# A seventh-product pair more, a fourth raw buffer, two reordered output blocks and spread transposes in a two-layer hybrid encoder

## The chip, the cores and the metric

The kernel runs on one core of one Trainium2 chip, as one program. Its time is the device time of one execution in microseconds. The kernel before has a median of 2345.92 us over three runs (2344.45 to 2348.73). Everything is float32; matrix products are taken as three products of a high and a low part in the fp32r type.

## The reference

Two layers, each of three residual sub-layers on 512 tokens of width 1024. Cut to what matters here:

```
h = h + 0.5 * post(SwiGLU(pre(h)))                 # FFN 1, hidden width 2816
u = pre(h); proj = u @ w_in
qa, ka, va, qb, kb, vb, qc, kc, vc, gl = split(proj)
  A: neighbourhood attention, 8 heads, with a bias table per head
  B: sliding-window attention, 8 query heads, 2 key heads, rotary, sink logit
  C: differential attention, 4 heads, two softmax maps each, rotary
gates = sigmoid(gl + b_gate)                       # 3 branches x 1024 columns
merged = sum_n gates[n] * (branch_n @ w_branch[n])
h = h + post(merged @ w_out)
h = h + 0.5 * post(SwiGLU(pre(h)))                 # FFN 2
```

All weights are read once from DRAM, 128x128 blocks in the order in which the kernel uses them. `gl` makes 24 column blocks of 128: 8 for each branch, called ga0 to ga7, gb0 to gb7 and gc0 to gc7 below.

## The kernel before, in words

Activations are held transposed, 1024 features by 512 tokens. Each layer goes through the stages FFN 1, projection (`project`), mixer (`mixer`) and FFN 2. TensorE is named PE below, VectorE DVE, ScalarE ACT, GpSimd POOL; SP is the queue that issues most transfers.

**Two ways to make a column block.** The direct way (`dense`, `mm3`, L322 to L324) takes eight row blocks of the weight, three products each, on 512 tokens: 24 matmuls of 512 columns for a column block of 128. The other way (`Seven`) takes a pair of column blocks together, as a two-by-two matrix of quadrants, by seven products in place of eight (Strassen's scheme in Winograd's form). Each product is 12 matmuls of 256 columns (`product`, L687), so a pair is 84 matmuls. For it the weights are added and split on DVE and ACT first: `sum13` (L628), `high1`, `low1` (L637), `high13`, `low13` (L647), `sum2` (L651), `high12` (L657), `low12` (L661), `sum4` (L665), `high24` (L669) and `low24` (L674). The accumulators are read back by `seed` (L726), `copy7` (L731), `copy2` (L735), `add21` (L740) and `add22` (L745). The loop over groups is a software pipeline: while group g is multiplied, group g+1 is prepared and the weights of group g+2 are asked for.

**Raw weights** come in tiles of 512 KB into a ring `wr` of three buffers (`fetch`, L206). A group takes two of them. A buffer comes free when the last of these DVE and ACT instructions has read it.

**The projection** makes 6 column blocks directly and 13 pairs by `Seven`: 12 pairs of q, k and v, and the pair gc6, gc7. Results are turned, rotated or split on DVE and ACT in tiles of a ring `t` of 16 buffers of 2 KB a partition, and stored to DRAM by POOL. `tables_of_a` also loads what the first two bias tables of attention A need; `biases` builds them (L1750, in tiles `edges`).

**The mixer** follows a written order, the string `ORDER`: qa0, aa0 and so on load and run attention heads, ga0 is a directly made gate block, fc0 to fc3 finish the four heads of attention C, and ya, yb, yc multiply a branch's output by a column block of `w_branch`. A gate block is 24 matmuls of 512 columns, a y block 12. A tile scheduler orders the instructions of each engine by this order and by when it takes operands to be ready, so gates and y blocks stand between the pieces of the attention heads. Gates of the branches B and C are stored to DRAM and read back when their y block is due.

**The first FFN** also keeps x: `keep` (L908 to L911) turns hT back by transposes on PE into a single PSUM bank `o`, ACT evicts it into a tile of the ring `t` of four buffers, and SP stores it to DRAM. These calls stand in a list `later`, of which two entries are taken at each weight step of the dense products.

Of the kernel before, what the change touches and what calls it, by code (L numbers as in the profile page):

```python
# [2 lines left out]

# [1 line left out]

# [5 lines left out]
F32 = mybir.dt.float32  # L11
# [29 lines left out]
COVER = (QA, KA, VA, QA + 1, KB, VB)  # L41
GROUPS = (
    (QA + 2, KA + 1), (VA + 1, KA + 2), (VA + 2, VA + 3), (QA + 3, KA + 3), (QB, QB + 1), (QB + 2, QB + 3), (QC, KC), (QC + 1, KC + 1), (VC, VC + 1), (QC + 2, KC + 2), (QC + 3, KC + 3), (VC + 2, VC + 3),
) + tuple((GL + i, GL + i + 1) for i in (22,))

COLS = {}
NCOLS = 0
# [21 lines left out]


ORDER = """
qa0 qa1 aa0 gb0 gb1 qa2 aa1 ga0 gb2 qa3 aa2 ga1 kb qb0 aa3 ga2 ga3 qb1 lc0 ab0 gb3 qb2 ab1 gb4 gb5 qb3 ab2 gb6 gb7 qc0 ab3 ga4 ga5 qc1 ac0 ga6 ga7 ya0 gc0 qc2 fc0 ac1 ya1 gc1 ya2 gc2 ya3 fc1 qc3 ac2 gc3 ya4 ya5 ya6 ya7 yb0 fc2 ac3 gc4 yb1 gc5 yb2 yb3 fc3 yb4 yb5 yb6 yb7 yc0 yc1 yc2 yc3 yc4 yc5 yc6 yc7
"""


# [39 lines left out]
def encoder_kernel(ctx: ExitStack, tc: tile.TileContext, order, xT, wts, cols, rows, rpb, consts, tables, out):  # L115
# [9 lines left out]
    BUFS = {"X": 6, "n": 2, "wr": 3, "wp": 2, "wq": 2}  # L125
    WP = BUFS["wp"] + BUFS["wq"]
    SKEW = 80
    ABUFS = {"f": {"t": 4, "x": 10}, "p": {"t": 16, "x": 10, "rr": 2}, "m": {"t": 5, "h": 4, "rr": 2, "tx": 5, "st": 14, "gd": 2, "g": 10, "s": 2, "pt": 4}}
    PBUFS = {"mm": 2, "mx": 2, "at": 3, "o": 1}

    def open_phase(kind):
# [10 lines left out]
    def nm(s):  # L142
        serial[0] += 1
        return f"{s}{serial[0]}"
# [15 lines left out]
    def f(t):  # L160
        return t.bitcast(F32)
# [36 lines left out]
    def holder(tag):  # L198
        return lambda: [big(tag, F32R, (P, HB, P), name="w") for _ in range(2)]

    def fetch(parts, eng=None):
        raw = sb.tile([P, WB, P], F32, tag="wr", name=nm("wr"), bufs=BUFS["wr"])
        src = wts[len(stream["raw"])].rearrange("p (a b) -> p a b", b=P)
        for c in range(0, WB, WB // parts):
            cs = slice(c, c + WB // parts)
            (eng or stream["eng"]).dma_start(raw[:, cs, :], src[:, cs, :])  # L206
        stream["raw"].append(raw)
# [373 lines left out]
    class Seven:  # L581


        def __init__(self, z, count):
            self.z, self.count = z, count
            self.hi, self.lo, self.raw = {}, {}, {}
            self.raws, self.W = {}, {}
            self.groups = [{} for _ in range(count)]
            self.seeds = None

        def quadrants(self, n):
            for i in range(2):
# [21 lines left out]
        def fetches(self, g):  # L614
            if g < self.count:
                self.W[g] = {}
                for _ in range(2):
                    fetch(1, nc.sync)
                self.raws[g] = [t.rearrange("p (a b) c -> p a b c", a=2) for t in stream["raw"][-2:]]

        def wpair(self, name):
# [2 lines left out]
        def sum13(self, g):  # L624
            w, r = self.W[g], self.raws[g]
            w["r13"] = sb.tile([P, 2, HB, P], F32, tag="wp", name=nm("r13"), bufs=BUFS["wp"])
            base = r[1][:, 1].unsqueeze(1).to_broadcast([P, 2, KD // 2, P])
            V.tensor_tensor(out=w["r13"], in0=base, in1=r[0], op=ALU.add)  # L628

        def high1(self, g):  # L630
            self.W[g]["h1"] = self.wpair("h1")
# [39 lines left out]
        def low24(self, g):  # L671
            w = self.W[g]
            w["l24"] = self.wpair("l24")
            V.tensor_tensor(out=w["l24"], in0=self.raws[g][1], in1=f(w["h24"]), op=ALU.subtract)  # L674


        def seed_banks(self, x):
# [87 lines left out]
    def ffn(l, which, X, accs):  # L765
# [104 lines left out]
        def at(fn, *args):  # L870
            return lambda: fn(*args)
# [13 lines left out]
        if first:  # L885
            s = Squares()
            for hs in HALVES:
                for b in range(KD):
                    s.add(V, hT[:, b, hs], hs)
            rB = pair("rB", F32)[:, 0, :]  # L890
            u1 = dense1(gu, l, KF + 1, X.blocks, tag="at", midway=lambda: finish_rms(s, rB))
            prepare(rowt)
            n = [sb.tile([P, 2, HK, HT], F32, tag="n", name=nm("n"), bufs=BUFS["n"]) for _ in range(2)]
            own = [sb.tile([P, 2, HK, HT], F32R, tag="X", name=nm("X"), bufs=BUFS["X"]) for _ in range(2)]
            quadrants(n)

            def normal(b):
                V.scalar_tensor_tensor(
                    out=n[b // HK][:, :, b % HK, :], in0=two(hT[:, b, :]), scalar=gcol(b), in1=two(rB),
                    op0=ALU.mult, op1=ALU.mult,  # L900
                )

            def keep(tb):
                d = dr.tile([P, D], F32, tag="kept", name=nm("kept"), bufs=2 * NT)
                for i in range(2):
                    tp = bank("o")
                    for k in range(HB):
                        PE.transpose(tp[:, k * P : (k + 1) * P], hT[:, HB * i + k, tb * P : (tb + 1) * P], ident)  # L908
                    t = big("t", name="h")
                    A.activation(t, tp, AF.Copy)  # L910
                    nc.sync.dma_start(d[:, i * T : (i + 1) * T], t)  # L911
                kept.append(d)

            stream["pace"] = 2
            for b in range(0, KD, 2):
                later.append(some(at(normal, b), at(normal, b + 1)))
            later.append(at(divide, "11", own[0][:, 0], own[1][:, 0]))
            later.append(at(divide, "22", own[0][:, 1], own[1][:, 1]))
            later.extend(at(keep, tb) for tb in range(NT))
            later.append(at(gap, "gaph", 48))  # L920
        else:
            quadrants(X.raw)
            for i, j in ((0, 0), (1, 0), (1, 1)):
                k = f"{i + 1}{j + 1}"
                hi[k], lo[k] = X.hi[i][:, j], X.lo[i][:, j]
# [11 lines left out]
                at(S.low1, 0),  # L937
            )
        )
        if not first:  # L940
            u1 = dense1(gu, l, KF + 1, X.blocks, tag="at")
        finish(0, g0, u0)
# [427 lines left out]
    def project(l, op, accs):  # L1370
# [264 lines left out]
        other(count - 1)  # L1635
        now()
        work(len(slowly))
        return made

    def raw_of(l, hd):  # L1640
# [78 lines left out]
    def mixer(l, op, made):  # L1719
# [15 lines left out]
        def biases(hd):  # L1735
            raw = raws.pop(hd)
            if hd < 2:
                edge = made["edges"][:, hd, :]
                mid = made["edges"][:, 2, 2 * P * hd : 2 * P * (hd + 1)]
            else:  # L1740
                edge = big("g", name="bedge")
                if hd % 2 == 0:
                    mids.append(big("g", name="bmid"))
                mid = mids[-1][:, 2 * P * (hd % 2) : 2 * P * (hd % 2) + 2 * P]

            def put(dst, mask, n0, n1):

                src = raw[:, 7 * RPBW + 39 - 8 * n0 :]
                (ps0, pn), _ = src.ap
                V.tensor_tensor(  # L1750
                    out=dst.rearrange("p (d r c) -> p d r c", r=8, c=8),
                    in0=bass.AP(src.tensor, src.offset, [[ps0, pn], [-8, n1 - n0], [-RPBW, 8], [-1, 8]]),
                    in1=mask.rearrange("p (d r c) -> p d r c", r=8, c=8),
                    op=ALU.add,
                )

            put(edge[:, 0:256], masks[0], 0, 4)
            put(mid, masks[1], 0, 4)
            put(edge[:, 256:384], masks[2][:, :P], 2, 4)
            put(edge[:, 384:512], masks[2][:, P:], 0, 2)  # L1760
            return lambda i: edge[:, 0:256] if i == 0 else edge[:, 256:512] if i == NT - 1 else mid


# [214 lines left out]
        def do(u):  # L1978
            kind, i = u[:2], int(u[2:] or 0)
            if kind == "fc" or kind[0] == "y":  # L1980
                if kind == "fc" and i >= len(oc) or kind[0] == "y" and (kind[1], 3) not in OT:
                    settle()
            if kind == "lc":
                first.update((c + i, begun(c + i)) for c in (QC, KC))
            elif kind == "lq":
                first[QC + i] = begun(QC + i)
            elif kind == "lk":
                first[KC + i] = begun(KC + i)
            elif kind == "tr":
                tables_in()  # L1990
            elif kind == "qa":
                held[u] = qkv_a(i)
            elif kind == "kb":
                tables_in()
                held["kb"] = qkv_b(KB), values(VB)
            elif kind == "qb":
                held[u] = qkv_b(QB + i)
            elif kind == "qc":
                held[u] = qkv_c(i)
            elif kind == "aa":  # L2000
                attn_a(i, *held.pop(f"qa{i}"))
            elif kind == "ab":
                attn_b(i, held.pop(f"qb{i}"), *held["kb"])
            elif kind == "ac":
                attn_c(*held.pop(f"qc{i}"))
            elif kind == "fc":
                finish_c(i)
            elif kind[0] == "g":
                gates("abc".index(kind[1]), i)
            elif kind[0] == "y":  # L2010
                combine("abc".index(kind[1]), kind[1], i)
# [146 lines left out]
```

## Time and profile before

| what | us |
|---|---|
| median of three runs | 2345.92 |
| the profiled execution | 2345.54 |
| its span | 2343.7 |
| PE busy in it | 2329.0 |
| DVE busy | 1917.7 |
| ACT busy | 1455.2 |
| first projection's seven-product loop, first to last L687 | 379.9 to 512.7 |
| second projection's, first to last L687 | 1540.4 to 1675.0 |

The span runs from the first to the last instruction, and the execution's own time is 1.84 us longer. Matmul ends are modelled and overlap: a matmul is shown as longer than the distance to the next one, so a busy share of 99% does not say that PE never waits. How many matmuls begin within a stretch says more. A chain row such as "PE mm L687 x24" with its duration gives this distance: 24 of them follow each other in that time.

### The profile page before, as it was taken

What the parts mean: (1) busy time and instruction counts of PE and PEld (TensorE: products, weight loads), DVE (VectorE), ACT (ScalarE), POOL (GpSimd) and SP (SyncE); (2) the same over time, 40 slices, a digit from 0 to 9 for tenths busy, and PEclk for the clock granted to TensorE, in tenths of its full rate; (3) what the DMA queues carried; (4) which work ended last, traced back from release to release, by engine and by line L of the source; (5) the groups of instructions that cost most, each with busy time, mean ns of one, the idle gap of its engine ahead of it and who ended that gap; (6) DMA issues with size and microseconds to landing.
All of it is one profiled execution on the core that took longest, in us unless ns stands there. A gap on an engine that the chain in (4) does not pass through costs nothing.

```text
span 2343.7 us, 40580 instructions
## 1 busy us (share of the span) xinstructions
PE 2329.0 (99%) x15278; PEld 2104.4 (90%) x15278; DVE 1917.7 (82%) x3103; ACT 1455.2 (62%) x2734; POOL 235.7 (10%) x378
## 2 busy tenths in 40 slices
PE   9999999999999999999999999999999999999998
PEld 7999889998888889998899998899988888999987
DVE  8987988868987778888888878798689776888796
ACT  6565566668766465655665555666687764656563
POOL 0111001110122001110001100011102110011100
PEclk9999999999999999999999999999999999999999
DMA  5566446668556425665536565276775664356642
GB/s 190 148 172 194 147 150 194 200 218 241 150 179 214 149 96 151 168 160 161 171 103 165 166 171 197 92 219 197 231 221 147 187 207 142 97 162 171 180 142 92
DMA packets 135636, 395.18 MB, mean 169 GB/s; under 512 B 19216, under 2 KB 23952, under 8 KB 134928
## 3 DMA queue, kind: packets, MB, share of 16 engines
q1 hardware_dynamic: 99712, 260.11, 35.8%
q0 software_dynamic: 22080, 84.95, 13.3%
q10 hardware_dynamic: 13648, 47.53, 6.6%
q8 instruction: 120, 1.97, 0.4%
q14 instruction: 76, 0.62, 0.1%
HBM read 326.98 MB, written 80.74 MB: 174 GB/s over the span
## 4 chain that ended last, share of the span: by engine, by line
PE 88%; DMA 4%; DVE 3%; issue 2%; ACT 1%; SPq 0%; POOL 0%; ACTq 0%; DVEq 0%; POOLq 0%
PE mm L687 20%; PE mx L687 10%; PE mm L1155 8%; PE mm L323 6%; PE mm L322 6%; PE mm L324 6%; PE mx L1155 5%; PE at L687 5%; PE at L1155 5%; DMA wr<-in_wts_dram 2%; PE at L322 2%; PE at L323 2%; PE at L324 2%; PE o L1155 1%; PE mx L1677 1%
## 5 line engine op out<-in xcount | busy, mean ns | idle before, releaser
L687 PE MATMUL mm<-X,h 128*128 128x256 f32 x1600 | 285.5, 278 | 2.3 <-DVE v L745 2.2
L687 PEld LDWEIGHTS mm<-X,h 128*128 128x128 f32 x1600 | 243.1, 188 | 4.3 <-DVE v L745 3.4
L687 PE MATMUL mm<-ht,h 128*128 128x256 f32 x800 | 224.0, 280 | 1.0 <-ACT at L726 1.0
L687 PE MATMUL mm<-ht,l 128*128 128x256 f32 x800 | 223.6, 279 | 0.0
L687 PE MATMUL mm<-lt,h 128*128 128x256 f32 x800 | 222.8, 278 | 0.0
L687 PE MATMUL mx<-ht,h 128*128 128x256 f32 x800 | 221.6, 277 | 0.4 <-ACT v L731 0.2
L687 PE MATMUL mm<-X,l 128*128 128x256 f32 x800 | 221.5, 277 | 0.0
L687 PE MATMUL mx<-ht,l 128*128 128x256 f32 x800 | 221.2, 276 | 0.0
L687 PE MATMUL mx<-lt,h 128*128 128x256 f32 x800 | 221.2, 276 | 0.0
L219 ACT ACTIVATE w<-wr 128x512 fp32r<-128x512 f32 x240 | 148.1, 626 | 96.4 <-PE mm L324 54.7
L220 DVE TENSOR_TENSOR w<-wr,w 128x512 fp32r<-128x512 f32 x240 | 163.0, 687 | 49.6 <-ACT w L219 48.6
L322 PE MATMUL mm<-X,w 128*128 128x512 f32 (+1 forms) x516 | 196.3, 380 | 0.3 <-ACT w L219 0.3
L323 PE MATMUL mm<-X,w 128*128 128x512 f32 (+1 forms) x516 | 195.4, 379 | 0.2
L324 PE MATMUL mm<-X,w 128*128 128x512 f32 (+1 forms) x516 | 193.6, 375 | 0.0
L637 DVE TENSOR_TENSOR l<-wr,h 128x1024 fp32r<-128x1024 f32 x100 | 122.4, 1224 | 67.8 <-PE mm L687 67.6
L669 ACT ACTIVATE h<-wr 128x1024 fp32r<-128x1024 f32 x100 | 106.2, 1062 | 84.1 <-PE mx L687 56.1
L687 PE MATMUL at<-X,w 128*128 128x256 f32 x1200 | 153.7, 277 | 0.0
L687 PEld LDWEIGHTS mm<-ht,h 128*128 128x128 f32 x800 | 150.7, 188 | 1.6 <-ACT at L726 1.4
L687 PEld LDWEIGHTS mx<-ht,h 128*128 128x128 f32 x800 | 150.3, 188 | 1.1 <-ACT v L731 1.0
L687 PEld LDWEIGHTS mm<-ht,l 128*128 128x128 f32 x800 | 150.8, 188 | 0.3 <-DVE l L674 0.2
L687 PEld LDWEIGHTS mm<-lt,h 128*128 128x128 f32 x800 | 150.7, 188 | 0.0
L687 PEld LDWEIGHTS mx<-lt,h 128*128 128x128 f32 x800 | 150.3, 188 | 0.0
(462 smaller groups left out, 6767.0 us busy)
## 6 DMA issues: line engine op xcount, KB each, us to landing
wr<-in_wts_dram SPq DMA_DIRECT2D x284, 512.0 KB, 3.7
wr<-in_wts_dram ACTq DMA_DIRECT2D x90, 512.0 KB, 4.2
sum<-in_wts_dram POOLq DMA_DIRECT2D x64, 512.0 KB, 5.1
st<-part SPq DMA_DIRECT2D x120, 128.0 KB, 4.2
ap<-in_wts_dram SPq DMA_DIRECT2D x20, 512.0 KB, 6.0
a<-kept SPq DMA_DIRECT2D x32, 256.0 KB, 6.3
ap<-sum SPq DMA_DIRECT2D x16, 512.0 KB, 3.3
x<-part SPq DMA_DIRECT2D x32, 256.0 KB, 3.6
```

The source lines that it names most:

```text
L219: A.activation(hi, raw, AF.Copy)
L220: V.tensor_tensor(out=lo, in0=raw, in1=f(hi), op=ALU.subtract)
L322: PE.matmul(acc, w[0], x[0], start=start, stop=False)
L323: PE.matmul(acc, w[0], x[1], start=False, stop=False)
L324: PE.matmul(acc, w[1], x[0], start=False, stop=stop)
L637: V.tensor_tensor(out=w["l1"], in0=self.raws[g][0], in1=f(w["h1"]), op=ALU.subtract)
L669: A.activation(self.W[g]["h24"], self.raws[g][1], AF.Copy)
L687: PE.matmul(acc, ws[i], xs[j], start=start and k == m == 0, stop=stop and k == n - 1 and m == 2, skip_group_check=True,)
L1155: PE.matmul(acc, x[i], w[j], start=start and n == 0, stop=stop and n == 2, skip_group_check=True)
L1677: PE.matmul(shaped(sp, k), qs, k, start=m == 0, stop=m == 1)
```

## The change

- `GROUPS` gets the pair gc4, gc5 ahead of gc6, gc7: 14 pairs by `Seven` in each projection. `ORDER` loses gc4 and gc5, and gc2 and gc3 move one place back: gc2 from behind fc0 to behind ac2, gc3 from behind ac2 to behind ac3.
- In `ORDER`, ya7 stands after ac3 and yb1 to yb4 all stand ahead of fc3.
- In the projection the second raw tile of every odd group goes to a buffer `wx` of its own, in the projection's pool. The ring `t` there shrinks from 16 to 14 buffers to make room (two buffers of 2 KB a partition against one of 4 KB).
- `sum13` of a group is put behind the last `low24` on DVE in the projection, and the bias tables of attention A behind the projection's last `low24`.
- In the first FFN the four `keep` calls no longer stand together in `later`; each alternates with one of the calls that prepare the `Seven` operands.

```diff
-) + tuple((GL + i, GL + i + 1) for i in (22,))
+) + tuple((GL + i, GL + i + 1) for i in (20, 22))
...
-... qc2 fc0 ac1 ya1 gc1 ya2 gc2 ya3 fc1 qc3 ac2 gc3 ya4 ya5 ya6 ya7 yb0 fc2 ac3 gc4 yb1 gc5 yb2 yb3 fc3 yb4 yb5 ...
+... qc2 fc0 ac1 ya1 gc1 ya2 ya3 fc1 qc3 ac2 gc2 ya4 ya5 ya6 yb0 fc2 ac3 gc3 ya7 yb1 yb2 yb3 yb4 fc3 yb5 ...
...
-    ABUFS = {... "p": {"t": 16, "x": 10, "rr": 2}, ...}
+    ABUFS = {... "p": {"t": 14, "x": 10, "rr": 2}, ...}
...
-    def fetch(parts, eng=None):
-        raw = sb.tile([P, WB, P], F32, tag="wr", name=nm("wr"), bufs=BUFS["wr"])
+    def fetch(parts, eng=None, raw=None):
+        if raw is None:
+            raw = sb.tile([P, WB, P], F32, tag="wr", name=nm("wr"), bufs=BUFS["wr"])
...
-                for _ in range(2):
-                    fetch(1, nc.sync)
+                for i in range(2):
+                    own = phase[0][0] == "p" and i and g % 2
+                    fetch(1, nc.sync, self.z("wx", F32, (P, WB, P)) if own else None)
...
-            V.tensor_tensor(out=w["r13"], in0=base, in1=r[0], op=ALU.add)
+            with tc.issue_after(self.last.ins) if self.last and phase[0][0] == "p" else nullcontext():
+                V.tensor_tensor(out=w["r13"], in0=base, in1=r[0], op=ALU.add)
...
-            V.tensor_tensor(out=w["l24"], in0=self.raws[g][1], in1=f(w["h24"]), op=ALU.subtract)
+            self.last = V.tensor_tensor(out=w["l24"], in0=self.raws[g][1], in1=f(w["h24"]), op=ALU.subtract)
...
-            later.extend(at(keep, tb) for tb in range(NT))
...
+        if first:
+            for tb in range(NT):
+                later.insert(len(later) - 10 + tb, at(keep, tb))
...
+            with tc.issue_after(made["last"].ins):
+                all_parts()
```

**SP's queue in the first projection.** The transfers `sh` are the rotary halves of a block; the others are raw weights. Before:

```order
L206 DMA wr740_4806<-in_wts_dram 128x1024
L206 DMA wr741_4808<-in_wts_dram 128x1024
L206 DMA wr756_4935<-in_wts_dram 128x1024
L1456 DMA sh751_4878<-x739_4802 32x512 x4
L1456 DMA sh753_4886<-v727_4725 32x512 x4
L206 DMA wr757_4937<-in_wts_dram 128x1024
L206 DMA wr772_5067<-in_wts_dram 128x1024
L1456 DMA sh767_5010<-x755_4931 32x512 x4
```

With the change:

```order
L207 DMA wr740_4806<-in_wts_dram 128x1024
L207 DMA wr741_4808<-in_wts_dram 128x1024
L207 DMA wr756_4935<-in_wts_dram 128x1024
L207 DMA wx757_4937<-in_wts_dram 128x1024
L1461 DMA sh751_4878<-x739_4802 32x512 x4
L1461 DMA sh753_4886<-v727_4725 32x512 x4
L207 DMA wr772_5067<-in_wts_dram 128x1024
L207 DMA wr773_5069<-in_wts_dram 128x1024
```

The second tile of an odd group now goes ahead of the eight `sh` transfers behind which it stood, into a buffer of its own.

**DVE at the first projection's second group.** `wr_4130` or `wx_4130` is that group's second tile, `wr_4222` and `wr_4224` the third group's. Before:

```order
L665 TENSOR_TENSOR wr_4130<-wr_4130 128x512
L745 TENSOR_TENSOR v_4173<-mm_4136,v_4173 128x256
L1750 TENSOR_TENSOR edges_5100<-pre_5095 128x256 x2
L1750 TENSOR_TENSOR edges_5100<-pre_5095 128x128
L674 TENSOR_TENSOR l_4258<-wr_4130,h_4238 128x1024
L628 TENSOR_TENSOR r_4263<-wr_4224,wr_4222 128x1024
```

With the change:

```order
L668 TENSOR_TENSOR wx_4130<-wx_4130 128x512
L1466 TENSOR_TENSOR x_4047<-x_4047,sh_4049 128x512
L748 TENSOR_TENSOR v_4173<-mm_4136,v_4173 128x256
L664 TENSOR_TENSOR w_4305<-wr_4224,w_4305 128x512
L677 TENSOR_TENSOR l_4258<-wx_4130,h_4238 128x1024
L631 TENSOR_TENSOR r_4263<-wr_4224,wr_4222 128x1024
```

The three bias instructions (`edges`) no longer stand ahead of `low24` (L674, now L677). All eight of the first two heads now stand behind the last group's `low24`.

**ACT in the first FFN, where x is kept.** h is a tile of the ring `t` that a transposed half of x goes into, w a split weight, t a half-finished FFN block in the same ring. Before:

```order
L910 ACTIVATE h80_463<-o79_458 128x512
L219 ACTIVATE w98_544<-wr86_493 128x512
L910 ACTIVATE h82_471<-o81_466 128x512
L206 DMA wr111_611<-in_wts_dram 128x1024
L854 ACTIVATE t83_486<-t83_486 128x512
L910 ACTIVATE h90_504<-o89_499 128x512
L219 ACTIVATE w102_564<-wr101_562 128x512
L910 ACTIVATE h92_512<-o91_507 128x512
```

With the change:

```order
L220 ACTIVATE w89_512<-wr82_477 128x512
L207 DMA wr111_611<-in_wts_dram 128x1024
L857 ACTIVATE t79_470<-t79_470 128x512
L913 ACTIVATE h86_489<-o85_484 128x512
L220 ACTIVATE w99_551<-wr98_549 128x512
L601 ACTIVATE ht390_515<-n57_358 128x1024
L913 ACTIVATE h88_497<-o87_492 128x512
L220 ACTIVATE w105_584<-wr98_549 128x512
```

Before, two tiles h are evicted ahead of t83; now the pair h86, h88 stands behind t79 and takes the ring's first two buffers again.

More of the change, by code (lines that the diff above doesn't have):

```diff
@@ L1 @@
 import math
-from contextlib import ExitStack
+from contextlib import ExitStack, nullcontext
 import numpy as np
@@ L71 @@
 ORDER = """
-qa0 qa1 aa0 gb0 gb1 qa2 aa1 ga0 gb2 qa3 aa2 ga1 kb qb0 aa3 ga2 ga3 qb1 lc0 ab0 gb3 qb2 ab1 gb4 gb5 qb3 ab2 gb6 gb7 qc0 ab3 ga4 ga5 qc1 ac0 ga6 ga7 ya0 gc0 qc2 fc0 ac1 ya1 gc1 ya2 gc2 ya3 fc1 qc3 ac2 gc3 ya4 ya5 ya6 ya7 yb0 fc2 ac3 gc4 yb1 gc5 yb2 yb3 fc3 yb4 yb5 yb6 yb7 yc0 yc1 yc2 yc3 yc4 yc5 yc6 yc7
+qa0 qa1 aa0 gb0 gb1 qa2 aa1 ga0 gb2 qa3 aa2 ga1 kb qb0 aa3 ga2 ga3 qb1 lc0 ab0 gb3 qb2 ab1 gb4 gb5 qb3 ab2 gb6 gb7 qc0 ab3 ga4 ga5 qc1 ac0 ga6 ga7 ya0 gc0 qc2 fc0 ac1 ya1 gc1 ya2 ya3 fc1 qc3 ac2 gc2 ya4 ya5 ya6 yb0 fc2 ac3 gc3 ya7 yb1 yb2 yb3 yb4 fc3 yb5 yb6 yb7 yc0 yc1 yc2 yc3 yc4 yc5 yc6 yc7
 """
@@ L127, in encoder_kernel @@
     SKEW = 80
-    ABUFS = {"f": {"t": 4, "x": 10}, "p": {"t": 16, "x": 10, "rr": 2}, "m": {"t": 5, "h": 4, "rr": 2, "tx": 5, "st": 14, "gd": 2, "g": 10, "s": 2, "pt": 4}}
+    ABUFS = {"f": {"t": 4, "x": 10}, "p": {"t": 14, "x": 10, "rr": 2}, "m": {"t": 5, "h": 4, "rr": 2, "tx": 5, "st": 14, "gd": 2, "g": 10, "s": 2, "pt": 4}}
     PBUFS = {"mm": 2, "mx": 2, "at": 3, "o": 1}
@@ L588, in __init__ @@
             self.groups = [{} for _ in range(count)]
-            self.seeds = None
+            self.seeds = self.last = None
         def quadrants(self, n):
@@ L1637, in project @@
         work(len(slowly))
+        made["last"] = S.last
         return made
@@ L1755, in put, with all_parts @@
                 )
[L1757 to L1760, printed above, removed]
+            def all_parts():
+                put(edge[:, 0:256], masks[0], 0, 4)
+                put(mid, masks[1], 0, 4)
+                put(edge[:, 256:384], masks[2][:, :P], 2, 4)
+                put(edge[:, 384:512], masks[2][:, P:], 0, 2)
+            with tc.issue_after(made["last"].ins):
+                all_parts()
             return lambda i: edge[:, 0:256] if i == 0 else edge[:, 256:512] if i == NT - 1 else mid
@@ L1982, in do @@
                     settle()
-            if kind == "lc":
+            if kind == "se":
+                settle()
+            elif kind == "lc":
                 first.update((c + i, begun(c + i)) for c in (QC, KC))
```

## The prediction

> **What bounds the kernel now.** I read the page first, for which engine sets the time.
>
> ```profile
> span 2343.7 us, 40580 instructions
> PE 2329.0 (99%) x15278; PEld 2104.4 (90%) x15278; DVE 1917.7 (82%) x3103; ACT 1455.2 (62%) x2734; POOL 235.7 (10%) x378
> PEclk9999999999999999999999999999999999999999
> ```
>
> PE is never long without work and its granted clock stays at full, so time goes down only by fewer matmuls or by shorter waits of PE, and there is little of the second. The chain of waits gives the price of a matmul; the groups kept apart by shape say which shape it is.
>
> ```profile
> 76.02 2.80 PE mm L687 x24
> 85.61 2.80 PE mm L687 x24
> 243.47 10.99 PE mx L1155 x48
> L687 PE MATMUL mx<-ht,h 128*128 128x256 f32 x151 | 41.7, 276 | 0.0
> L1155 PE MATMUL mx<-wh,f 128*128 128x512 f32 x32 | 10.1, 390 | 0.0
> L322 PE MATMUL mm<-X,w 128*128 128x512 f32 x65 | 25.8, 397 | 0.0
> ```
>
> Two neighbouring groups of the seven products in FFN 1 begin 85.61 − 76.02 = 9.59 us apart: 84 matmuls of 256 columns, 114 ns each. 48 matmuls of 512 columns take 10.99 us, 229 ns each. A gate's matmuls (L322) have that second shape.
>
> Then I read how long the seven-product loops take: over 19 groups of the second layer's FFN 1, and over the 13 of each projection (16 of these matmuls a group), with the transposes that stand among the projection's.
>
> ```profile
> L687 PE MATMUL mm<-X,h x304: 276/276/383, 1209.7 to 1392.5; 128*128 128x256 f32 x152
> L687 PE MATMUL mm<-X,h x208: 276/276/388, 379.9 to 512.7; 128*128 128x256 f32 x104
> L687 PE MATMUL mm<-X,h x208: 276/276/388, 1540.4 to 1675.0; 128*128 128x256 f32 x104
> L1434 PE MATMUL at<-cons,x x24: 271/273/329, 380.7 to 508.2; 128*128 128x128 f32 x24
> L1434 PE MATMUL at<-cons,v x8: 272/272/328, 480.5 to 508.6; 128*128 128x128 f32 x8
> 41.23 0.44 PE o L908 x4
> ```
>
> The FFN's pace is 182.8 / 19 = 9.62 us a group. 13 groups would be 125.1 us, and 32 transposes at 0.11 us (four take 0.44) add 3.5: 128.6. The projections take 132.8 and 134.6, so 4.2 and 6.0 us, 10.2 together, are lost there. What ended PE's waits, from the same view and from PE's time line, with the chain ahead of the longest:
>
> ```profile
>   DVE v L745: 1.8, 4
>   ACT at L726: 2.4, 3
> 1629.37 5.56 DMA wr<-in_wts_dram
> 1634.95 1.23 DVE L628 TENSOR_TENSOR r<-wr,wr 128x1024 f32<-128x1024 f32 x1 [1.16 <-DMA wr<-in_wts_dram]
> 1635.01 0.64 ACT L657 ACTIVATE w<-wr 128x512 fp32r<-128x512 f32 x1 [2.47 <-DMA wr<-in_wts_dram]
> 1636.91 0.39 PE L687 MATMUL mm<-ht,h 128*128 128x256 f32 x1 [1.00 <-ACT at L726]
> wr<-in_wts_dram SPq DMA_DIRECT2D x23, 512.0 KB, 3.8
> ```
>
> A raw weight is asked for at 1629.37 and lands 5.56 us later (the median of 23 is 3.8). DVE and ACT stand still for it, each in its own order, and `seed` (L726), queued on ACT behind two splits of the late tile, comes late to PE. The DMA is thus the real end of these waits, though PE's rows name DVE and ACT.
>
> **The change part by part.** The sum is made against the profiled execution's own 2345.5 us; the median of the runs shown is 0.4 above it.
>
> *The pair gc4, gc5.* The mixer loses 48 matmuls of 512 columns a layer, 11.0 us; the projection gains a group, 9.6 us. That is 1.4 a layer, **2.8 us gained**. Its splits go off the mixer's DVE and ACT and return as one group's share in the projection, weighed below. The Trainium skill speaks against it ("TensorE: Matmul & The Clock Gate", Back-to-back issue gap): in a sustained stream it gives about 131 ns a matmul at 512 columns and 81 at 128. Midway, 98 at 256 (my estimate from that page), 84 would take 8.2 us against 6.3 for 48, so the seven products would lose 1.9 us a pair. The rows above have 229 and 114 ns.
>
> *The fourth raw buffer and the two orderings.* With three buffers the first tile of group g+2 waits until `low24` of group g, and SP's queue holds later weights behind it and behind rotary transfers. With `wx`, every group takes buffers that the group two before it used, and the odd group's second tile passes the eight `sh` transfers. `sum13`, the first DVE instruction to stop for a late tile, no longer stands ahead of `low24`. What can be won is between nothing (the waits merely move) and all 10.2 us. PE's idle rows bound it nearer: those of the first projection and of the second.
>
> ```profile
> 380.00:513.00 133.00, 131.27 (x1129) 129.91 (x1127) 113.30 (x161) 86.28 (x162) 23.68 (x44) 1.00 0.66 212
> 1540.00:1675.00 135.00, 133.00 (x1128) 130.84 (x1127) 114.30 (x161) 86.61 (x162) 23.70 (x44) 1.00 0.66 209
> 398.17 0.63 ACT L1412 ACTIVATE hi<-x 128x512 fp32r<-128x512 f32 x1
> 399.01 0.69 DVE L1413 TENSOR_TENSOR lo<-x,hi 128x512 fp32r<-128x512 f32 x1
> ```
>
> The columns are length, then PE, PEld, DVE, ACT and POOL busy. Counted by busy time PE stands idle 1.7 and 2.0 us; the rest of the 10.2 are gaps shorter than a matmul is shown to last. DVE is busy 85% of these stretches. The added group brings it about a thirteenth of the 113, and 14 groups take at least 14 × 9.62 + 3.5 = 138.2 us of PE, so it comes to (113.3 + 8.7) / 138.2, 88%: not the bound, but with little room after a burst of rotations. The ring `t`, two shorter, also makes the `hi` written at 398.17 wait for a tile whose last reader ends at 399.70, 1.5 us of ACT in each layer, with a later split in the queue behind it. I take six tenths of the 10.2, **6.0 us gained**, nearer to all than to nothing because each longer wait has a late `wr` ahead of it.
>
> *The bias tables.* Eight DVE instructions a layer (L1750) go from the loop to its end.
>
> ```profile
> 380.00:513.00 133.00, 2.57 (x8) 1.00 0.66 212
> 508.09 0.42 DVE L740 TENSOR_TENSOR v<-mx,v 128x256 f32<-128x256 f32 x1 [4.01 <-PE mx L687]
> ```
>
> That row is of L1750 alone: 2.57 us of DVE. At the loop's end DVE idles 4.01 us ahead of the last `add21`, which covers it. I count zero; without that cover the first scores of attention A would wait up to 2.6 us a layer, and PE has two direct gates to do meanwhile.
>
> *x kept in spread steps.* PE is in order, and the sixth half of x to be turned finds its single bank `o` taken.
>
> ```profile
> 39.40 4.71 SPq L911 DMA_DIRECT2D kept<-h  x4
> 42.59 0.49 PE o L908 x4
> 43.16 0.61 ACT h L910
> 43.79 5.64 DMA kept<-h
> 49.53 0.61 ACT h L910
> 50.19 0.55 PE L908 MATMUL o<-cons,a 128*128 128x128 f32 x3 [1.60 <-ACT h L910]
> ```
>
> ACT could not evict the bank before 49.53, since its next tile h waited until a stored one had landed, 5.64 us after its issue. Spread, the same tiles come back over four weight steps in place of two (a step is 12 matmuls of 229 ns, 2.7 us): what must be won is 1.6 us, and 5.5 us more are there for it. The new place of h86 makes ACT wait for the first store (issued at 39.40; landed by about 45 at 5.64 us), behind which a split for matmuls at about 48 is queued, so 2 to 3 us of cover remain. **1.6 us gained**; the ends are 0 and 1.8.
>
> *The mixer's order.* Nothing but the gates' 48 matmuls and their 4 splits on DVE and ACT (of 512 columns) is taken away, but filler moves between the heads of attention C. By the chain's price a gate is 5.5 us of PE and a y block 2.75. Behind ac1 stood three y blocks and two gates, 19.25 us, now three and one, 13.75; behind ac2 stood 19.25, now 16.5; behind ac3 19.25, as before. How full DVE is there:
>
> ```profile
> 668.00:697.00 29.00, 29.00 (x142) 23.67 (x140) 21.71 (x51) 21.85 (x43) 7.80 (x15) 1.00 0.59 175
> 697.00:727.00 30.00, 30.00 (x152) 24.79 (x151) 25.62 (x57) 21.02 (x41) 6.74 (x13) 1.00 0.69 202
> 1859.00:1890.00 31.00, 31.00 (x157) 25.65 (x156) 26.14 (x58) 21.37 (x41) 6.75 (x13) 1.00 0.71 197
> L220 DVE TENSOR_TENSOR w<-wr,w 128x512 fp32r<-128x512 f32 x42 | 28.7, 685 | 1.3 <-ACT w L219 1.3
> ```
>
> The zones run from the scores of ac1, ac2 (first and second layer) to the next head's. The fullest show DVE at 25.6 of 30 and 26.1 of 31, 85%, with PE never idle. Behind ac1 are left 29 − 5.5 = 23.5 us of PE's work and 21.7 − 2 × 0.685 = 20.3 of DVE's; behind ac2 27.25 and 25.6 − 2 × 0.685 = 24.2 (a split and a product of the y block). If 85% were the most that DVE can give, they would take 23.9 and 28.5, 0.4 and 1.3 late, 1.7 a layer. But PE filled these zones, so 85% is a floor of what DVE can give, not shown to be its limit; I take 1.2, nearer to 1.7 since DVE works in order: **2.4 us lost**. The ends are 0 and 8.25 a layer, all of the filler that these two zones lose.
>
> Sum: −2.8 − 6.0 − 1.6 + 2.4 = −8.0. 2345.5 − 8.0 = 2337.5, and with the 0.4 of the median **2337.9 us**, 0.34% faster.
>
> **Rivals.**
>
> *All waits go.* The projections run at the FFN's pace and the mixer keeps its own: −2.8 − 10.2 − 1.6, so 2331.3. For it: the FFN has the same loop, with three buffers, at 9.62. Against: the FFN has no rotations and no stacks on DVE.
>
> *The projection's waits move.* The late tile is not the buffer's fault but the transfer's: 3.8 us at the median with 66% of the DMA engines busy, and up to 5.56. Then the fourth buffer wins nothing: −2.8 − 1.6 + 2.4, 2343.9. For it: POOL's stores and SP's small transfers stay in the same stretch. Against: the transfer at 1629.37 was asked for late, and a request a group earlier would cover 5.56 with 9.6.
>
> *Attention C starves, slower.* If a head's chain of scores, maxima and exponentials, not DVE's load, sets the zone's length, PE stands idle for all the filler taken away: 8.25 a layer, 16.5 in place of 2.4. −2.8 − 6.0 − 1.6 + 16.5 = +6.1: 2352.0. It decides against the change from 5.2 us a layer on (10.4 / 2). For it: DVE at 87%. Against: in the zones of now PE has no idle time at all.
>
> *512 columns are cheaper than the rows say.* Each pair would lose 1.9 in place of winning 1.4, 6.6 us more in all: 2344.5. That is the skill's spacing, and the rows of this case speak against it throughout.
>
> **How the numbers follow.** What a measurement of this kernel can tell from no change is about 0.2%, 4.7 us: faster is below 2341.2, slower above 2350.6. Forecast 0.56 (its own range 2334 to 2342), all waits go 0.12, the waits move 0.20, starvation 0.08, cheap 512 columns 0.01, and 0.03 for something else. Faster: 0.52 of the forecast, 0.12, and 0.06 of the third case, where a part is still won: 0.70. Slower 0.08, same 0.22. The range runs from the second case to the third, 2331 to 2344.5, and leaves out starvation.
>
> **What would show it.** Right: L687's first to last in the projections at 140 to 142 us for 14 groups (138.2 is the floor, 142.4 and 144.2 what the old losses would give); no idle of 1 us ahead of L726 there; no idle ahead of L908; the mixer from its first score to the first `w_out` matmul about 10 us shorter. Wrong: idle rows of PE ahead of attention C's matmuls, the zones from ac1 on no shorter, or ACT waiting in the projection for POOL's stores on the shorter ring.

## The result: slower by 0.64%, and where the profile after has it

| | before | changed |
|---|---|---|
| median, us | 2346.06 (6 runs beside it) | 2360.14 (6 runs, 2358.97 to 2363.52) |
| ratio, 95% interval | | 1.0064 (1.0054 to 1.0074) |
| the profiled execution, its span | 2345.54, 2343.7 | 2359.82, 2358.0 |

The forecast was 2337.9, so 22.2 us are missing. The page of the changed kernel gives the same picture as that of before: PE at 99% and a clock row of nines.

```profile
span 2358.0 us, 40762 instructions
PE 2327.6 (99%) x15350; PEld 2110.6 (90%) x15350; DVE 1923.6 (82%) x3113; ACT 1467.0 (62%) x2742; POOL 236.4 (10%) x378
PEclk9999999999999999999999999999999999999999
```

A slice is 59 us, so a stop of 3 or 8 us does not show there. By stages it does. The seven-product loops, from the view of their line (count, durations, first and last start), are those of the first and the second projection:

```profile
L690 PE MATMUL mm<-X,h x224: 276/276/386, 377.9 to 518.9; 128*128 128x256 f32 x112
L690 PE MATMUL mm<-X,h x224: 276/276/286, 1547.0 to 1686.6; 128*128 128x256 f32 x112
```

That is 141.0 us for 14 groups, inside the 140 to 142 that were forecast, and 139.6, 0.4 below them; the first loop starts 2.0 us sooner (379.9 before). The mixer was to become 10 us shorter. Its first score matmul and its first `w_out` matmul, before and then changed, from PE's time line (start, length):

```profile
512.88 0.28 PE L1677 MATMUL mx<-early 128*128 128x256 f32 x1
795.74 0.40 PE L322 MATMUL at<-w,hi 128*128 128x512 f32 x1
```

```profile
519.11 0.40 PE L1683 MATMUL mx<-early 128*128 128x256 f32 x2
803.06 0.40 PE L323 MATMUL at<-w,hi 128*128 128x512 f32 x1
```

It went from 282.9 to 283.9 us (in the second layer from 283.2 to 284.6). With 11.0 us of matmuls gone and 1.2 allowed for the order, 273.1 and 273.4 were forecast: 10.8 and 11.2 us are missing in the two mixers, 22.0 of the 22.2. Where they are missing, the start of attention C's first score matmul tells, before and then changed:

```profile
L1876 PE MATMUL mx<-st,st x32: 387/394/496, 641.1 to 745.8; 128*128 128x512 f32 x32
```

```profile
L1886 PE MATMUL mx<-st,st x32: 387/394/500, 659.7 to 758.8; 128*128 128x512 f32 x32
```

From there to the first `w_out` matmul the time went from 154.6 to 143.4 us in the first layer (154.7 to 143.9 in the second), so the gates' 11.0 us are won there in full. Ahead of it, in attention A and B, it went from 128.2 to 140.6 (128.5 to 140.7). The waits of PE over the two mixers of the changed kernel (engine, line, what it waited for, us in total, times, longest), first and second layer:

```profile
PE mx L1683 <- DVE nmx L1686: 7.2, 1, 7.2
PE mx L1683 <- DMA st<-part: 2.6, 1, 2.6
```

```profile
PE mx L1683 <- DVE nmx L1686: 8.0, 1, 8.0
PE mx L1683 <- DMA st<-part: 2.5, 1, 2.5
```

Before, the same question gave 0.2 us in the first mixer. The second mixer has one wait more, of 0.3 us. Stop 1 ends at 536.5 and stop 2 at 648.7, both while attention A and B are computed (the first score of attention C starts at 659.7); in the first layer's attention C there is none. Behind each the clock is halved. Windows laid on the records of the granted clock (start and end, length, busy time and count of PE, PEld, DVE, ACT and POOL, the granted clock, DMA share, GB/s):

```profile
536.80:540.20 3.40, 3.40 (x16) 3.11 (x15) 0.42 (x1) 0.39 (x1) 0.00 (x0) 0.50 1.00 296
646.10:652.80 6.70, 4.05 (x12) 3.48 (x13) 4.58 (x16) 1.99 (x4) 0.00 (x0) 0.50 0.37 110
1813.50:1820.00 6.50, 2.99 (x9) 2.70 (x10) 4.16 (x15) 1.53 (x4) 0.00 (x0) 0.50 0.41 112
```

The records are 3.41 us long behind the short stop and 6.83 behind the long one, in both layers. PE does half its work in what it is busy of them, so stop 1 costs 2.6 + 1.7 and stop 2 7.2 + 2.0 (the record begins before PE is back). Together 13.5 us in the first layer, 13.8 in the second: counted off like this, the mixers would take some 270.5 us. Kernels below that have neither stop take 273.1 to 273.6, of which 0.9 to 1.5 are other waits, so this count is some 1.6 us too high.

**Stop 1** begins on SP's queue. Its time line at the mixer's start, before and then changed; a row with x4 runs from the first to the last of the four loads of bias rows:

```profile
491.01 25.83 SPq L1733 DMA_DIRECT2D braw<-in_rpb_dram  x4
517.01 0.50 SPq L1795 DMA_DIRECT2D st<-part  x1
```

```profile
493.61 33.17 SPq L1739 DMA_DIRECT2D braw<-in_rpb_dram  x4
526.88 0.50 SPq L1805 DMA_DIRECT2D st<-part  x1
```

The loads `st` for the third head of attention A start 4.1 us behind the first score before, 7.8 us behind it now. SP's own waits in the changed kernel say why, and POOL's time line what it waits for:

```profile
SPq L1739 <- DMA gate<-x: 26.3, 1, 26.3
```

```profile
520.08 0.54 POOL L1570 DMA_DIRECT2D gate<-x  x1 [5.82 <-ACT x L1390]
```

The second bias load stands 26.3 us for the store of the last group's first gate block to DRAM, which POOL issues at 520.08, after the last product. It goes out at 524.7 (508.9 before). Of the `st` loads queued behind it, the last that PE needs is asked for at 529.98 and lands 6.37 us later, and PE goes on at 536.48. In the program's memory map that gate's tile lies at bytes 138240 to 140287 of each partition, and the bias load's buffer at 136512 to 138559: they share 320 bytes. Before, no tile of the last group lay there. (The Trainium skill, "DMA: Bandwidth & Descriptors", Anatomy of one DMA — SWDGE (gpsimd) path, says that a DMA engine itself never waits for a semaphore: the sequencer that issues the transfer does, ahead of handing it over. The row of 26.3 on SP's queue agrees.)

**Stop 2** is VectorE's. The time lines of SP and of VectorE in the changed kernel:

```profile
638.65 1.71 SPq L1784 DMA_DIRECT2D sh<-raw  x4
639.10 0.67 DVE L1791 TENSOR_TENSOR x<-x,cosR 128x512 f32<-128x512 f32 x1
647.58 0.69 DVE L1792 TENSOR_TENSOR sh<-sh,sinR 128x512 f32<-128x512 f32 x1 [7.81 <-DMA sh<-raw]
```

and before:

```profile
617.61 2.22 SPq L1774 DMA_DIRECT2D sh<-raw  x4
635.64 0.68 DVE L1781 TENSOR_TENSOR x<-x,cosR 128x512 f32<-128x512 f32 x1
636.84 0.69 DVE L1782 TENSOR_TENSOR sh<-sh,sinR 128x512 f32<-128x512 f32 x1
```

The rope of the second head of attention C multiplies `sh`. Before, its loads were asked for 19 us ahead of it; now they are asked for at 638.65 (their buffer comes free with a store of a split C tile, 6.93 us under way from 631.67), VectorE reaches the rope at 639.8, and scores of attention B stand behind it. Counted from each mixer's start the loads are 14.8 us later (+104.7, now +119.5) and the rope 2.8 us earlier (its first product +122.8, now +120.0). The order tells the same: the rope stands behind 60 of the 64 score reductions of attention A and B, before behind all 64, and the two splits of the first C head, whose stores free the buffers for these loads, behind 48 and 56 of the 64 softmax exponentials of A and B on ScalarE, before behind 44 and 52.

### The profile page after: what moved, and what is told of

It is laid out like the page before. It is cut to its first block, busy times and chain, and to the rows that moved or that the text cites. A ratio compares the mean times of both kernels' runs of the same rounds, so it can differ in the third digit from the quotient of the medians.

```text
span 2358.0 us, 40762 instructions
## 1 busy us (share of the span) xinstructions
PE 2327.6 (99%) x15350; PEld 2110.6 (90%) x15350; DVE 1923.6 (82%) x3113; ACT 1467.0 (62%) x2742; POOL 236.4 (10%) x378
## 4 chain that ended last, share of the span: by engine, by line
PE 93%; DMA 3%; DVE 2%; ACT 1%; issue 1%; SPq 0%; POOL 0%; DVEq 0%; ACTq 0%
PE mm L690 23%; PE mx L690 11%; PE mm L1160 7%; PE mm L325 6%; PE mm L323 6%; PE mm L324 6%; PE at L690 6%; PE mx L1160 5%; PE at L1160 5%; PE at L324 2%; PE at L323 2%; PE at L325 2%; PE o L1160 1%; PE mx L1683 1%; PE at L1714 1%; PE o L1717 1%
## 5 line engine op out<-in xcount | busy, mean ns | idle before, releaser
L690 PE MATMUL mm<-X,h 128*128 128x256 f32 x1632 | 290.5, 278 | 1.4 <-DVE v L748 1.4
L690 PEld LDWEIGHTS mm<-X,h 128*128 128x128 f32 x1632 | 247.9, 188 | 2.6 <-DVE v L748 2.0
L221 DVE TENSOR_TENSOR w<-wr,w 128x512 fp32r<-128x512 f32 x232 | 157.1, 686 | 45.2 <-ACT w L220 44.1
L323 PE MATMUL mm<-X,w 128*128 128x512 f32 (+1 forms) x484 | 185.3, 383 | 0.9 <-ACT w L220 0.9
L220 ACT ACTIVATE w<-wr 128x512 fp32r<-128x512 f32 x232 | 143.1, 628 | 69.2 <-PE mm L325 30.3
L324 PE MATMUL mm<-X,w 128*128 128x512 f32 (+1 forms) x484 | 183.7, 380 | 0.1
L325 PE MATMUL mm<-X,w 128*128 128x512 f32 (+1 forms) x484 | 183.6, 379 | 0.0
L690 PEld LDWEIGHTS mm<-X,l 128*128 128x128 f32 x816 | 153.4, 188 | 0.0
```

The source lines that it names most:

```text
L220: A.activation(hi, raw, AF.Copy)
L221: V.tensor_tensor(out=lo, in0=raw, in1=f(hi), op=ALU.subtract)
L323: PE.matmul(acc, w[0], x[0], start=start, stop=False)
L324: PE.matmul(acc, w[0], x[1], start=False, stop=False)
L325: PE.matmul(acc, w[1], x[0], start=False, stop=stop)
L690: PE.matmul(acc, ws[i], xs[j], start=start and k == m == 0, stop=stop and k == n - 1 and m == 2, skip_group_check=True,)
```

## The experiments

All of them compute the whole result. Times are medians, each ratio is against runs of the kernel before on the same chip.

**x_elsewhere: the last gate gathered in another buffer.** The instructions of all engines stand in the same order as in the changed kernel; only one address differs.

```diff
-            groups[g]["t"] = big("t", name="x")
+            if g + 1 < count:
+                groups[g]["t"] = big("t", name="x")
+            else:
+                groups[g]["t"] = z("wx", F32, (P, WB, P)).rearrange("p a b -> p (a b)")[:, :T]
```

> The changed kernel with one edit: the last group's first gate block is gathered in the fourth raw buffer, which is free by then and lies under attention C's outputs, and not in the buffer that lies under the second bias row load. Order of instructions on all engines unchanged. Theory (the last gate's store holds SP's queue at the mixer's start, and stop 2 is partly its lateness carried on): the second bias load is asked for before 510 and not at 524.67, the wait of 2.6 us for the restacked loads and its 3.41 us at half clock go in both layers (some 8.7 us in all), and the loads of the second C head come some 4 to 5 us sooner, so that the wait of 7.2 and 8.2 us at the rope falls to about 3; time 2342 to 2351. Rival (the new order of the mixer's units loses the time, the waits are only where it shows): the time stays at 2358 to 2360, with the waits moved elsewhere.

2347.54 us, ratio 1.0009 (1.0000 to 1.0018). SP's time line, and then PE's waits in the first and the second mixer:

```profile
493.97 19.36 SPq L1742 DMA_DIRECT2D braw<-in_rpb_dram  x4
513.43 0.50 SPq L1808 DMA_DIRECT2D st<-part  x1
```

```profile
PE mx L1686 <- DVE nmx L1689: 4.8, 1, 4.8
```

```profile
PE mx L1686 <- DVE nmx L1689: 5.3, 1, 5.3
```

The second bias row is asked for at 499.0, stop 1 is gone in both layers, and 12.9 us with it ((1.0064 − 1.0009) × 2345.9; by the two intervals, some 3 us more or less). So 320 shared bytes cost more than the whole change was to bring. Stop 2 fell by 2.4 and 2.7 us, less than the 4 to 5 expected: part of it was stop 1's lateness handed on, most was its own.

**pair_alone: the second pair and nothing else.**

```diff
-) + tuple((GL + i, GL + i + 1) for i in (22,))
+) + tuple((GL + i, GL + i + 1) for i in (20, 22))
-... fc2 ac3 gc4 yb1 gc5 yb2 yb3 fc3 ...
+... fc2 ac3 yb1 yb2 yb3 fc3 ...
```

> The kernel before with the second pair of gates by seven products alone: its two blocks taken out of the mixer's order, every other unit in its old place; no fourth raw buffer, x kept in one step, old bias tables. Theory (the mixer's preparation of the C heads is redrawn by the 14th group itself, not by the new mixer order): the rope of the second C head stands behind 60 scores instead of 64 and waits 3 to 8 us in each layer for its loads; 2346 to 2356, while the projection alone would give 2343. Rival (the new mixer order is at fault): no such wait, 2342 to 2345.

2369.13 us, ratio 1.0107 (1.0091 to 1.0123), worse than both. PE's waits in the first mixer, and VectorE's from 600 to 660 us:

```profile
PE mx L1677 <- DVE nmx L1680: 6.9, 1, 6.9
PE mm L322 <- DVE x L1942: 1.3, 2, 0.8
PE at L1912 <- ACT sqt L1909: 1.2, 1, 1.2
```

```profile
DVE sh L1782 <- DMA sh<-raw: 7.6, 1, 7.6
```

There is no stop 1 (that needs the pair and the shorter ring together: raw_buffer_alone, with the ring alone, has none either) and all of stop 2. The order says the same, 60 scores and 48 and 56 exponentials as in the changed kernel, while it keeps 64, 44 and 52 with the other parts alone. This run adds the group and takes two gate blocks out of the mixer's order, behind ac3. The orders of two programs that were built and not run separate the two: 13 groups without gc4 and gc5 in the mixer keep 64, and 14 groups with both still in it have 60. So the 14th group moves the preparation of the C heads, more than a hundred microseconds behind the place that was changed. PE's other rows are new: behind the last C unit PE waits for the head's finish, and at 778.1 the clock is halved for 6.83 us. This is starvation as the prediction had it in a rival, in a kernel without the new order and at another place: the rival had it behind ac1 and ac2. It is why the time lies above the 2346 to 2356 that were expected.

**x_elsewhere_old_order: everything but the new mixer order.** The order is that of pair_alone, the rest that of x_elsewhere.

> The kernel of run x_elsewhere with the old mixer order less the two gate blocks (what run pair_alone had). Theory (in pair_alone the two removed gate blocks leave TensorE short of cover behind the last C unit, and the new order mends just that): idle of 4 to 5 us and 6.83 us at half clock near 770 to 780 in each layer, 2357 to 2364. Rival (that stop came from the old buffers): 2346 to 2349. The prediction's own term for the new order was a loss of 2.4 us: by it this run would be 2345.

2364.52 us, ratio 1.0086 (1.0073 to 1.0100). PE's waits, first mixer:

```profile
PE mx L1686 <- DVE nmx L1689: 5.0, 1, 5.0
PE mm L323 <- DVE x L1955: 1.3, 2, 0.8
PE at L1925 <- ACT sqt L1922: 1.2, 1, 1.2
```

The same rows behind the last C unit, with half-clock records of 3.41 us (first layer) and 6.83 (second), and 17 us more than x_elsewhere (2347.5), 0.5 above the range that was expected. The new order, with gc3 and two y blocks more between ac3 and the last finish, is worth that much once the gates are gone.

**raw_buffer_alone: the fourth raw buffer with its two orderings, the bias tables' among them.** 13 groups, the old order, x kept in one step (the parts of the diff on `fetch`, `fetches`, `sum13`, `low24`, `biases` and the ring `t`).

> The kernel before with the fourth raw buffer and the sums and bias tables queued behind the low parts, alone: 13 groups, old mixer order, x kept in one step. Theory and the prediction's term agree: the seven-product loop loses about 3 us less in each layer, 2340 (2338.5 to 2342). Rival (the bias tables behind the last low part hold up the mixer's first scores): the loop gains but the mixer gives back up to 2.6 us a layer, 2344 to 2346.

2337.10 us, ratio 0.9964 (0.9952 to 0.9977).

```profile
L690 PE MATMUL mm<-X,h x208: 276/276/388, 379.4 to 509.9; 128*128 128x256 f32 x104
L690 PE MATMUL mm<-X,h x208: 276/276/388, 1537.6 to 1668.3; 128*128 128x256 f32 x104
```

130.5 and 130.7 us against 132.8 and 134.6: 6.2 us gained in the loops, where 6.0 of 10.2 was the term. The median lies 1.4 us below the expected range, 8.0 under the median of before beside it; the profiled execution (2339.04) is 6.5 under that of before. Where the medians have more than the loops' 6.2 is open. The mixers stay at 283.0 and 282.8, so the bias tables behind the last low part cost nothing.

**keep_alone: x kept in spread steps.**

```diff
-            later.extend(at(keep, tb) for tb in range(NT))
...
+        if first:
+            for tb in range(NT):
+                later.insert(len(later) - 10 + tb, at(keep, tb))
```

> The kernel before with the four keeps of x spread over the last steps of the first FFN's list, alone. Theory: the first seven-product group starts 2.0 us sooner as in the changed kernel and all behind it moves with it, 2344.1 (2343.3 to 2344.9). Rival (the gain is taken up by the next wait): 2346.

2343.06 us, ratio 0.9989 (0.9980 to 0.9998). The first seven products start at 67.1 in place of 68.7, 1.6 us sooner, and the 2.1 us of the medians are about what the theory asked for; the interval reaches from 0.5 to 4.7. But the profiled execution (2345.70, the slowest of eleven) doesn't carry the gain to the end: its second projection loop takes 137.1 us against 134.6, so that its last seven products start at 2223.5, before at 2223.3. The rival is not excluded.

**raw_and_keep: the last two together, without the pair.**

> The kernel before with the fourth raw buffer and its orderings and the keeps of x spread, no pair: 13 groups and the old mixer order. Theory (the parts add): 2345.1 - 8.0 - 2.1 = 2335, against 2345 before; a rival (the keeps' gain is part of the other's): 2337.

2337.03 us, ratio 0.9966 (0.9954 to 0.9978), the time of the buffer alone and the 2337 of the rival. Whether the 2.1 us are in it cannot be told: the interval is 5.6 us wide.

**x_elsewhere_qc1_late: the second C head prepared later.**

```diff
-... qc0 ab3 ga4 ga5 qc1 ac0 ga6 ...
+... qc0 ab3 ga4 ga5 ac0 qc1 ga6 ...
```

> The kernel of run x_elsewhere with the second C head's preparation one unit later in the mixer's list, behind attention C's first unit. Its rope then stands behind all 64 scores of attention A and B, not 60. Theory (what is left of stop 2 is the place of this rope on VectorE ahead of its loads): the idle of 4.8 and 5.3 us and the 3.41 and 6.83 us at half clock behind it go, 2332 to 2337; if the later preparation then starves the second C unit, some of it comes back there. Rival (the stop is the loads' lateness, whatever stands at VectorE): the wait moves behind the same loads, 2345 to 2349.

2367.94 us, ratio 1.0099 (1.0085 to 1.0113). PE's waits, first mixer:

```profile
PE at L1925 <- ACT sqt L1922: 2.3, 2, 1.2
PE mm L323 <- DVE x L1955: 2.2, 2, 1.4
PE at L1912 <- DVE nm L1892: 1.4, 1, 1.4
```

The rope's wait is gone from PE and from VectorE. But it is 20 us slower than x_elsewhere, and not where the expectation had put "some of it": the second C unit (683.9) waits 0.6 us in the first layer and 2.7 in the second. Most of the idle, 7.0 us in the first layer, and three records of halved clock (13.7 us) stand between 740 and 784, at the last C unit and the finishes behind it. The place of the rope is a cause, and the later place is no cure.

**x_elsewhere_qc0_early: the first C head prepared earlier.**

```diff
-... qb3 ab2 gb6 gb7 qc0 ab3 ...
+... qb3 ab2 qc0 gb6 gb7 ab3 ...
```

> The kernel of run x_elsewhere with the first C head's preparation two gate blocks earlier in the mixer's list, so that its split on ScalarE stands behind 24 softmax exponentials instead of 30; the second head's rope stands behind 62 and 64 scores. Theory: its stores end and the second head's loads start some 8 us sooner and the rope finds them there; both the idle and the half clock go, 2332 to 2337. Rival (the place on VectorE alone decides and two scores are too few): 2340 to 2347.

2337.57 us, ratio 0.9968 (0.9956 to 0.9981), 9.6 us under x_elsewhere. The time lines of SP and VectorE, and all of PE's waits in the first mixer:

```profile
618.47 1.71 SPq L1787 DMA_DIRECT2D sh<-raw  x4
632.90 0.68 DVE L1794 TENSOR_TENSOR x<-x,cosR 128x512 f32<-128x512 f32 x1
639.91 0.68 DVE L1795 TENSOR_TENSOR sh<-sh,sinR 128x512 f32<-128x512 f32 x1
```

```profile
PE mm L323 <- DVE x L1955: 1.5, 1, 1.5
```

The loads are asked for 21 us ahead of the product that needs them (the first head's splits stand behind 40 and 52 exponentials, the rope behind 62 and 64 scores). Nothing is left of stop 2, and the mixers take 273.4 and 273.6 us: the 273.1 and 273.4 of the forecast. With the two stops mended the changed kernel is at the forecast of 2337.9. The run moves the loads and the rope together, so it doesn't say how much of stop 2 each was. And raw_and_keep, with no pair at all, is at 2337.0.

**settle_earlier and block_later: the one stop that is left.** VectorE's time line of x_elsewhere_qc0_early at it:

```profile
763.61 0.16 DVE L1927 TENSOR_SCALAR msc<-at 128x4 f32<-128x4 f32 x1 [2.87 <-PE at L1925]
764.30 0.68 DVE L1955 SCALAR_TENSOR_TENSOR x<-x,mm 128x512 f32<-128x512 f32 x1
```

VectorE stands for the third C head's sum of squares, and the y block whose reading frees the PSUM bank for PE is queued behind it.

```diff
-... ac2 gc2 ya4 ya5 ya6 yb0 fc2 ac3 gc3 ya7 yb1 ...
+... ac2 gc2 ya4 ya5 se ya6 yb0 fc2 ac3 gc3 ya7 yb1 ...   (settle_earlier; se runs the head's second half)
+... ac2 gc2 ya4 ya5 yb0 fc2 ac3 gc3 ya6 ya7 yb1 ...      (block_later)
```

> The kernel of run x_elsewhere_qc0_early with the second half of the third C head written one output block earlier in the mixer's list (ahead of ya6), so that its sum of squares is ready before VectorE comes to it. Theory (the one stop over 0.5 us that is left, 1.65 us a layer near 765 and 1921, is VectorE waiting for that sum with the freeing of a PSUM bank queued behind it): the stop goes, 3.3 us less than 2337.6: 2334 (2332 to 2336). Rival (the earlier second half meets attention's own softmax and starves there): 2338 to 2342.

> The kernel of run x_elsewhere_qc0_early with one output block (ya6) moved from ahead of the third head's finish to behind the last C unit's gate: one block less ahead of the third finish, one more behind the last unit. Theory: the stop at 765 stays or grows by the 2 us that the block covered, 2337 to 2343; rival (the last unit lacks cover more than the third finish): 2333 to 2336.

2336.33 us, ratio 0.9958 (0.9946 to 0.9971), the lowest time of all, and 2340.73, ratio 0.9971 (0.9960 to 0.9982). PE's waits in the first mixer of settle_earlier:

```profile
PE o L1916 <- DVE lo L350: 0.7, 1, 0.7
PE mm L323 <- DVE x L1955: 0.2, 1, 0.2
```

and of block_later, with the clock behind them:

```profile
PE mm L323 <- DVE x L1955: 1.5, 1, 1.5
PE at L1925 <- ACT sqt L1922: 0.5, 1, 0.5
```

```profile
769.10:772.30 3.20, 3.20 (x9) 2.51 (x8) 1.98 (x3) 0.63 (x1) 0.00 (x0) 0.50 0.00 0
```

The stops went as the theory had it: that of 1.5 us falls to 0.2, with one of 0.7 in another place, where the sum comes earlier, and is joined by a second one where a block of cover is taken away. The time of settle_earlier did not: it is 1.2 us less in the medians, where 3.3 were expected, and the intervals don't separate it from x_elsewhere_qc0_early or from raw_buffer_alone. Two of the seven executions of block_later took 2336.2 and 2336.4 us at a mean clock of 0.999, the other five 2340.7 to 2342.4 at 0.997 or 0.998; the profile is of one of the five.

## Why the prediction was wrong, point by point

- **The pair, −2.8.** The profiles without the two stops bear out the sign and about half of the size. From raw_and_keep to settle_earlier the loops grow from 129.9 and 130.3 us to 139.2 and 139.6, and the mixers shrink from 283.1 and 283.0 to 273.1 and 273.1: 0.7 and 0.6 us gained for pair, order and mending together, where −1.4 and +1.2 a layer were forecast. In the medians it is 0.7 us in all, which the intervals don't separate from none. A group for 9.3 us against 10.0 speaks against the rival in which each pair loses 1.9.
- **The fourth raw buffer, −6.0.** Right: 6.2 in the loops with the buffer alone. In the changed kernel the loops lose 2.8 and 1.4 us above the floor of 138.2, 4.2 in all, as the term had it. That it fits to the tenth is luck: the same 14 groups with the fourth buffer took 139.2 to 141.6 us in the other profiled executions. And with the pair the buffer won less than 6.0: pair_alone, 14 groups on three buffers, has 140.8 and 141.7 us, 1.9 more in all than the changed kernel and 3.7 to 3.9 more than settle_earlier and x_elsewhere_qc0_early.
- **The bias tables, 0.** Right: no loss in raw_buffer_alone's mixers.
- **x kept, −1.6.** The wait ahead of L908 is gone, and the first group starts 2.0 us sooner in the changed kernel, 1.6 in keep_alone. Whether that reaches the end is open: the medians of keep_alone say so, its profiled execution and raw_and_keep don't.
- **The mixer's order, +2.4: one of the two steps that failed.** It said that nothing but the gates' matmuls and splits is taken away and that filler moves between the heads of attention C, and so it looked for a loss behind ac1 and ac2 alone. Stop 2 lies ahead of attention C's first score, where no unit was moved. The scheduler set the C heads' preparation anew because the projection has a group more, and pair_alone shows stop 2 with no unit moved; mending it was worth 9.6 us. Where the term did look, the changed kernel loses nothing: from attention C's first score on it is 11.2 and 10.8 us shorter, for 11.0 of matmuls taken away. Without stop 2 the same stretch takes 145.3 us (x_elsewhere_qc0_early) and 144.9 (settle_earlier) in the first layer, so 1.3 to 1.7 us are lost there after all, near the 1.2, but that is luck: the term had VectorE too full, at 85%, and at the one stop of 1.5 us VectorE itself stands idle for 2.87.
- **The ring `t`, two shorter: the other step that failed, and the dearer one.** The 1.5 us of ACT in the projection were counted. That the same ring is the memory under the mixer's first loads, and that 14 groups on 14 buffers put the last gate under the second bias load, was not looked at. Stop 1 and what it handed on were 12.9 us.
- The rest adds up: 12.9 for the shared bytes and 9.6 for the place of the first C head are 22.5, and 22.2 were missing; the intervals leave some 4 us either way, so the tenths agree by chance.
- **Attention C starves** (2352.0, 0.08) was the only rival that ended slower. Its sign came true by other causes. Its mechanism shows behind the last C unit, not in the two zones that it priced, and is what the new order prevents: 17 us without it. The 87% that it names is VectorE's load from 641 to 668 us (23.43 of 27), ahead of those two zones. **All waits go** and **the waits move** are both refuted by the loops' 4.2 us, the second by the time of raw_buffer_alone too.

What draws the scheduler's order from 64 to 60 when a group is added was not found out. That it is the added group is shown by the orders; by which operand's readiness is open.

## What to carry to other kernels

A change in the number of buffers or of groups also changes what lies under the next stage's first loads: compare, in the memory map, the tiles that are written last with the buffers that are loaded first, and look at what the issuing queue holds behind them. Where a scheduler sets the order, compare it over the whole stage, not only where units were moved, and check for each load that is waited for how far ahead of its reader it is asked for (19 us was enough here, 1 us was not). A stop of PE of some 2 us or more, and several shorter ones close together, are to be priced with the half clock that came behind them here.

## What the runs showed of the hardware that was not expected

The granted clock falls after stops much shorter than expected and in steps of one length. A single stop of 1.5 us left it at 1.00 (x_elsewhere_qc0_early, 765.1 to 772.0). Stops of 0.5 and 1.5 us within 3 us (block_later), of 2.0 (x_elsewhere_old_order, second layer, at 1881), of 2.5 and 2.6 (changed kernel) and of 4.8 (x_elsewhere) were followed by one record of 3.41 us at 0.50; of 5.0 (x_elsewhere_old_order), 5.3 (x_elsewhere, second layer), 6.1, 6.9, 7.2 and 8.0 by one of 6.83. The longest stop alone doesn't set the record: behind the last C unit, a row of stops of 0.2 to 1.2 us was followed by 6.83 in both layers of pair_alone, and by 3.41 and 6.83 in the two of x_elsewhere_old_order. The Trainium skill ("TensorE: Matmul & The Clock Gate", Part 1: The HAM clock gate) gives a free-running window of 3413 ns: the lengths agree, one window and two. It also says that the clock falls after at least one idle window of about 3.4 us; here 2.0 us of idle was enough, and the measured rows decide.
